# Four down-projection operands made one by one inside the next block, and the second logits product over all 128 rows

## The chip, the core and the metric

The kernel runs on one core of one Trainium2 chip. Its time is the device time of one launch in microseconds (us). The kernel before took 2153.45 us, the median of three runs (2152.48 to 2155.72). The engines are named as in the profile: PE is TensorE (PEld its weight loads), DVE is VectorE, ACT is ScalarE, POOL is GpSimd, and SP is SyncE, which issues the DMAs.

## The reference: one layer of a decoder trunk

The input x is 512 tokens of 2048 float32 values. What is computed, cut to what matters:

```python
h = rmsnorm(x, norm_mix)
proj = h @ w_in                                   # split into the inputs of three head groups
out_a = rmsnorm(swa_sink_attention(aq, ak, av, sinks, rel_bias))   # 12 heads, 4 key/value heads, window 128
out_b = rmsnorm(gla_chunked(bq, bk, bv, log_gate)) * silu(br)      # 4 heads, gated linear attention
out_c = rmsnorm(stick_breaking_attention(cq, ck, cv))              # 8 heads, strictly causal
x = x + concat(out_a, out_b, out_c) @ w_out
h = rmsnorm(x, norm_mlp)
x = x + square(relu(h @ w_mlp_in)) @ w_mlp_out    # 2048 -> 8192 -> 2048
out = rmsnorm(x, norm_final)
```

The heads are 64 wide. The logits of the two softmax-like groups are `q @ k.T` over these 64 values: `z` in the stick-breaking group, `logits` in the window group.

## The kernel before

**Products in parts.** Every float32 operand is split into a high part, rounded to the format that PE multiplies (`whi`, `sh`, `kh`), and a low part, the rest (`wlo`, `sl`, `kl`). ACT makes the high part by a copy, DVE the low part by a subtraction. A product is then three matmuls: high by high, high by low, low by high. The large products (query and key columns of the stick-breaking group, output projection, both MLP projections) go by a Strassen-like scheme with seven products per two-by-two block, named A11, S1, S2, A12, S3, S4 and A22; the sums of blocks that it needs are made by DVE (L174 is the helper `sub`, L171 `add`).

**Logits.** A head's 64 query rows and its 64 key rows are each loaded twice, into the lower and the upper 64 partitions (`twice`, L516). `split_q` (L522) leaves the high part of q in the lower half of `qh` and the low part in the upper half. `split_k` (L530) makes `kh`, the high part of k, on all 128 partitions, and `kl`, the low part, on the lower 64. `qk` (L537) then needs two matmuls: L539 multiplies all 128 rows of `qh` by `kh`, which sums the high and the low part of q against the high part of k; L540 multiplies the lower 64 rows of `qh` by `kl`. It is called once for each stick-breaking head and 128-query block (8 heads, 4 blocks, 256 to 512 key columns), followed there by a bf16 matmul that adds the mask (L564), and once for each window head and block (12 heads, 4 blocks, 256 key columns): 80 calls in all. `split_k` runs 12 times (8 stick-breaking heads and 4 key/value heads).

**Stages.** Input transposes and the first projections come first. The stick-breaking heads run in a software pipeline of six steps per head and block (load, split, logits, weights, transpose, values), beside the matmuls of other projections (L119 to L121); then the gated group; then the window heads in a like pipeline, beside the first output-projection products (L958 to L960). After them come the rest of the output projection, the up-projection (16 blocks `b` of 512 columns, L1261 to L1263) and the down-projection (8 groups `g`, L958 to L960).

**Down-projection operands.** Two up-projection blocks make the operands of one down-projection group. The results of a block are four tiles `a[i, j]` (tile name `av`). `down_half` (L1229) makes seven operands of them: A11 and S3 when the first block is done, A12 in the second block, and, when the second block is done, A22, S1, S2 and S4, one behind the other. `down_split` (L1221) makes one: a copy on ACT (L1224, `dh`), a subtraction on DVE (L1225, `dl`), and two DMAs to HBM (L1226, L1227), from which the down-projection reads them back (L1339). The parts `dh` and `dl` share a ring of two buffers.

**What sets the order.** The kernel is written with a tile framework. Its scheduler takes the instructions in the order of the program text, with their priorities (`tc.high_priority()` moves loads and weight splits ahead), their dependencies and the free buffers of each pool, and lays down one fixed list for each engine. Each engine works its list in order and waits on semaphores; where something stands on an engine is thus decided at build time.

Of the kernel before, what the change touches and what calls it, by code (L numbers as in the profile page):

```python
# [10 lines left out]
F32 = mybir.dt.float32  # L11
F32R = mybir.dt.float32r
# [3 lines left out]
ALU = mybir.AluOpType  # L16
# [7 lines left out]
HD = 64  # L24
# [39 lines left out]
def trunk(ctx, tc, x, norm_mix, w_in, sinks, rel_bias, gate_w, gate_b, gla_norm,  # L64
          swa_norm, sb_norm, w_out, norm_mlp, w1, w2, norm_final, hconst, honehot, out):
    nc = tc.nc
    V, S, G, T = nc.vector, nc.scalar, nc.gpsimd, nc.tensor
# [102 lines left out]
    def add(out_, a, b, eng=G):  # L170
        eng.tensor_tensor(out=out_, in0=a, in1=b, op=ALU.add)  # L171

    def sub(out_, a, b, eng=G):
        eng.tensor_tensor(out=out_, in0=a, in1=b, op=ALU.subtract)  # L174

    ORDER = ("A11", "S1", "S2", "A12", "S3", "S4", "A22")

    ORDER0 = ("A11", "A12", "S1", "S2", "S4", "S3", "A22")
# [91 lines left out]
    def qkh(name, shape=(P, 512), dt=F32):  # L270
        return own("qkh", 6, name, shape, dt)
# [24 lines left out]
    for q in range(4):  # L296
# [7 lines left out]
        for a in range(4):  # L304
# [3 lines left out]
            g = gT[:, 4 * q + a : 4 * q + a + 1]  # L308
# [137 lines left out]
    for g in range(2):  # L446
        sops = hops[g]
# [81 lines left out]

    def split_k(raw):  # L530
        kh = qkh("kh", dt=F32R)
        kl = qkh("kl", (HD, 512), F32R)
        S.activation(kh, raw, AF.Copy)
        V.tensor_tensor(out=kl, in0=raw[:HD], in1=kh[:HD].bitcast(F32), op=ALU.subtract)
        return kh, kl

    def qk(z, qh, qs, k, ks, last=True):  # L537
        kh, kl = k
        T.matmul(z, lhsT=qh[:, qs], rhs=kh[:, ks], start=True, stop=False, skip_group_check=True)  # L539
        T.matmul(z, lhsT=qh[:HD, qs], rhs=kl[:, ks], start=False, stop=last, skip_group_check=True)  # L540


    hd, oC = {}, {}
# [392 lines left out]
    def slot(pool, name, shape, dt=F32):  # L936
        return pool.tile(list(shape), dt, tag="s", name=name)
# [3 lines left out]

    def row_group(acc, sops, wsrc, k1, k2, done=None, order=ORDER, rscale=None, before=None):
        for np_ in range(2):
            raws = raw_tiles([wsrc[k : k + 512, n * 1024 + np_ * 512 : n * 1024 + np_ * 512 + 512]
                              for k in (k1, k2) for n in range(2)], rp)

            def quad(i, j, h):
                return raws[2 * (i - 1) + j - 1][:, 2 * h : 2 * h + 2]  # L950

            def mm(dst, s, wt, h, start, rows):
                (sh, sl, _), (wh, wl) = s, wt
                for u in rows:
                    us = slice(u * P, (u + 1) * P)
                    for k in range(2):
                        kc = 2 * h + k
                        T.matmul(dst[u], lhsT=sh[:, kc, us], rhs=wh[:, k], start=start and k == 0, stop=False, skip_group_check=True)  # L958
                        T.matmul(dst[u], lhsT=sh[:, kc, us], rhs=wl[:, k], start=False, stop=False, skip_group_check=True)  # L959
                        T.matmul(dst[u], lhsT=sl[:, kc, us], rhs=wh[:, k], start=False, stop=h == 1 and k == 1, skip_group_check=True)  # L960

            def after(p, X, Y, Z, rows):
                todo = {"A11": (X, 0, 0), "S1": (Z, 1, 1), "S2": (X, 0, 1), "A12": (Y, 0, 0),
                        "S3": (X, 1, 1), "S4": (Z, 0, 1), "A22": (X, 1, 0)}[p]
                bk, th, nh = todo
                for u in rows:
                    a = acc[2 * th + u][nh][:, np_ * 512 : np_ * 512 + 512]
                    if rscale:
                        V.scalar_tensor_tensor(out=a, in0=bk[u], scalar=rscale[2 * th + u], in1=a, op0=ALU.mult, op1=ALU.add)  # L969
                    else:  # L970
                        V.tensor_tensor(out=a, in0=bk[u], in1=a, op=ALU.add)
                if done:
                    done(p, np_, rows)

            strassen(quad, sops, mm, 2, after, order, None if np_ else before, by_rows=done and np_)


# [82 lines left out]
    with tc.high_priority():  # L1060
        sops, ready = mixed_operands(1536, 1024, lambda n: slot(s3, n, (P, 2, 512)), lambda n: slot(s1, n, (P, 2, 512)))
# [5 lines left out]
    acc = load_acc(lambda t, nh: x[t * P : (t + 1) * P, nh * 1024 : (nh + 1) * 1024])  # L1067
    row_group(acc, sops, w_out, 1536, 1024, before=first_ops)
    sops, ready = mixed_operands(0, 512)
# [135 lines left out]
    NG = DFF // 1024  # L1205
# [15 lines left out]
    def down_split(g, p, t, last=False):  # L1221
        hi = tp4.tile([P, 4, 256], F32R, tag="t1", name="dh", bufs=2)
        lo = t.bitcast(F32R) if last else tp4.tile([P, 4, 256], F32R, tag="t1", name="dl", bufs=2)
        S.activation(hi, t, AF.Copy)  # L1224
        V.tensor_tensor(out=lo, in0=t, in1=hi.bitcast(F32), op=ALU.subtract)  # L1225
        nc.sync.dma_start(dS[g][p][0], hi.bitcast(F32))  # L1226
        nc.sync.dma_start(dS[g][p][1], lo.bitcast(F32))  # L1227

    def down_half(b, th):  # L1229

        g, j = divmod(b, 2)
        a = quads
        if (j, th) == (0, 0):
            down_split(g, "A11", a[1, 1])
        elif (j, th) == (0, 1):
            sub(a[1, 1], a[1, 1], a[2, 1], V)
            down_split(g, "S3", a[1, 1])
        elif (j, th) == (1, 0):
            down_split(g, "A12", a[1, 2])
        else:  # L1240
            down_split(g, "A22", a[2, 2])
            add(a[2, 1], a[2, 1], a[2, 2], V)
            down_split(g, "S1", a[2, 1], True)
            sub(a[1, 1], a[2, 2], a[1, 1], V)
            down_split(g, "S2", a[1, 1])
            sub(a[1, 2], a[1, 2], a[1, 1], V)
            down_split(g, "S4", a[1, 2], True)

    for b in range(DFF // 512):
        raws = raw_tiles([w1[k * 512 : (k + 1) * 512, b * 512 : (b + 1) * 512] for k in range(4)], rp)  # L1250

        def wquad(i, j, h):
            return raws[2 * (i - 1) + h][:, :, (j - 1) * 256 : j * 256]

        def mm(dst, s, wt, h, start, rows):
            (sh, sl, _), (wh, wl) = s[h], wt
            for j in range(2):
                js = slice(j * P, (j + 1) * P)
                o = dst[0][:, j * 256 : (j + 1) * 256]
                for k in range(4):  # L1260
                    T.matmul(o, lhsT=wh[:, k, js], rhs=sh[:, k], start=start and j == 0 and k == 0, stop=False, skip_group_check=True)  # L1261
                    T.matmul(o, lhsT=wh[:, k, js], rhs=sl[:, k], start=False, stop=False, skip_group_check=True)  # L1262
                    T.matmul(o, lhsT=wl[:, k, js], rhs=sh[:, k], start=False, stop=h == 1 and k == 3, skip_group_check=True)  # L1263

        down_quads(b)
        done = []

        def view(th, nh):
            return quads[th + 1, b % 2 + 1][:, 2 * nh : 2 * nh + 2]

        def finish(th, nh):
            v = view(th, nh)
            S.activation(v, v, AF.Square)
            if th in done:
                down_half(b, th)
            done.append(th)

        def after(p, X, Y, Z, rows):
            bk = {"S1": Z, "S4": Z, "A12": Y}.get(p, X)[0].rearrange("p (j q) -> p j q", j=2)
            th, nh, first = {"A11": (0, 0, 1), "S1": (1, 1, 1), "S2": (0, 1, 1), "A12": (0, 0, 0),  # L1280
                             "S3": (1, 1, 0), "S4": (0, 1, 0), "A22": (1, 0, 1)}[p]
            v = view(th, nh)
            if p == "A22":
                S.activation(v, bk, AF.Relu)
            elif first:
                S.copy(v, bk)
            else:
                V.tensor_tensor(out=v, in0=bk, in1=v, op=ALU.add)
                S.activation(v, v, AF.Relu)
            if not first or p == "A22":  # L1290
                finish(th, nh)

        strassen(wquad, up_ops, mm, 1, after, *((ORDER0, up_operand) if b == 0 else ()), ahead=b > 0)
# [38 lines left out]
    r2 = [row_rms2(xsq, t) for t in range(NT)]  # L1332
# [10 lines left out]
    for g in range(NG):  # L1343
        sops = down_operands(g)
        if g == 0:
            acc = load_acc(lambda t, nh: dx2[t][nh])
        if g == NG - 1:
            pool = places.pop(0)
            for nh in range(2):
                gt = slot(pool[nh], "gfin", (P, 1024))  # L1350
                nc.sync.dma_start(gt, bcast(norm_final[nh * 1024 : (nh + 1) * 1024], 1024))
                gfin.append(gt)
        row_group(acc, sops, w2, g * 1024, g * 1024 + 512, *((y_done, ORDER0) if g == NG - 1 else (None, ORDER)), rscale=r2)


# [31 lines left out]
```

## Time and profile before

| | us |
|---|---|
| median of three runs | 2153.45 |
| the profiled execution, whole | 2151.19 |
| its span, first to last instruction | 2149.4 |
| PE busy in the span | 2076.6 (97%) |
| DVE busy | 1664.7 (77%) |
| ACT busy | 1039.8 (48%) |
| POOL busy | 97.7 (5%) |

The profile is of one execution. A matmul's shown end is modelled and the next one may start before it, so the pace of PE is read from one start to the next rather than from durations. "64\*128" in a row is the part of the PE array that an instruction uses, rows by columns. "x2" is two instructions merged into a row. In a list of waits, the engine that stood idle comes first, and what it waited for second. The mean granted clock of PE over the span is 0.988 of full speed.

### The profile page before, as it was taken

To read this page: it belongs to the slowest core of one execution; us is meant where nothing else is said; L and a number is where in the kernel's file an instruction comes from. 1 tells how busy PE (TensorE), PEld (TensorE's weight loads), DVE (VectorE), ACT (ScalarE), POOL (GpSimd) and SP (SyncE) were. 2 spreads that over 40 slices of the span, in tenths; PEclk is the share of its full clock that TensorE was granted. 3 is DMA by queue.
4 is the path that set the end of the run, shared out by engine and by line. 5 is a ranking of instruction groups with operands and counts; after the bars stand their busy time and mean duration, and the time that the engine had idled before them with its cause. 6 is when DMAs were issued, how large, how long until landed. Compare 5 with 4: busy or idle time off the path is not lost. (4 is left out here: it accounts for less than half of the span.)

```text
span 2149.4 us, 30666 instructions
## 1 busy us (share of the span) xinstructions
PE 2076.6 (97%) x12174; PEld 1786.0 (83%) x12174; DVE 1664.7 (77%) x1936; ACT 1039.8 (48%) x1500; POOL 97.7 (5%) x63
## 2 busy tenths in 40 slices
PE   8999999999899997999999999999999999999997
PEld 7997877777677776999999999999788888888876
DVE  7875554435677898788888888887998988988887
ACT  6435644323365465565565565555433333333334
POOL 1110000011200002000000000000000000000012
PEclk9999999999999999999999999999999999999999
DMA  6375333334532442464464554569766366455532
GB/s 227 114 173 147 109 126 106 120 116 146 182 103 82 164 143 83 157 236 177 176 224 179 186 206 181 190 217 374 264 229 241 136 218 234 167 205 216 196 117 79
DMA packets 180906, 373.17 MB, mean 174 GB/s; under 512 B 19800, under 2 KB 44186, under 8 KB 180762
## 3 DMA queue, kind: packets, MB, share of 16 engines
q1 hardware_dynamic: 180762, 371.20, 49.7%
q8 instruction: 96, 1.57, 0.3%
q14 instruction: 48, 0.39, 0.1%
HBM read 287.01 MB, written 84.15 MB: 173 GB/s over the span
## 5 line engine op out<-in xcount | busy, mean ns | idle before, releaser
L200 ACT ACTIVATE whi<-raw 128x1024 fp32r<-128x1024 f32 x532 | 561.7, 1060 | 682.5 <-PE X L960 239.5
L201 DVE TENSOR_TENSOR wlo<-raw,whi 128x1024 fp32r<-128x1024 f32 x532 | 647.2, 1227 | 152.6 <-ACT whi L200 152.0
L174 DVE TENSOR_TENSOR raw<-raw 128x1024 f32<-128x1024 f32 x304 | 369.8, 1230 | 31.0 <-DMA raw<-in_w_mlp_in 25.3
L1263 PE MATMUL X<-sh,wlo 128*128 128x256 f32 x1024 | 290.3, 284 | 10.8 <-DVE wlo L201 10.8
L1261 PE MATMUL X<-sh,whi 128*128 128x256 f32 x1024 | 289.9, 283 | 11.0 <-ACT whi L200 10.0
L1262 PE MATMUL X<-sl,whi 128*128 128x256 f32 x1024 | 288.3, 282 | 0.0
L959 PE MATMUL X<-wlo,sh 128*128 128x512 f32 x640 | 257.1, 402 | 2.8 <-DVE wlo L201 2.7
L960 PE MATMUL X<-whi,sl 128*128 128x512 f32 x640 | 256.1, 400 | 0.0
L958 PE MATMUL X<-whi,sh 128*128 128x512 f32 x640 | 233.8, 402 | 11.5 <-ACT whi L200 4.3
L1263 PEld LDWEIGHTS X<-sh,wlo 128*128 128x128 f32 x1024 | 195.2, 191 | 14.1 <-DVE wlo L201 14.1
L1261 PEld LDWEIGHTS X<-sh,whi 128*128 128x128 f32 x1024 | 195.4, 191 | 13.3 <-ACT whi L200 12.0
L1262 PEld LDWEIGHTS X<-sl,whi 128*128 128x128 f32 x1024 | 195.3, 191 | 0.0
L958 PEld LDWEIGHTS X<-whi,sh 128*128 128x128 f32 x640 | 121.3, 190 | 42.6 <-issue 6.2
L959 PEld LDWEIGHTS X<-wlo,sh 128*128 128x128 f32 x640 | 122.1, 191 | 33.6 <-DVE wlo L201 5.2
L960 PEld LDWEIGHTS X<-whi,sl 128*128 128x128 f32 x640 | 122.0, 191 | 28.8
L1262 PE MATMUL Z<-sl,whi 128*128 128x256 f32 x512 | 143.1, 280 | 2.3 <-DVE sl L1106 2.3
L1261 PE MATMUL Z<-sh,whi 128*128 128x256 f32 x512 | 143.3, 280 | 0.2 <-ACT whi L200 0.2
L1263 PE MATMUL Z<-sh,wlo 128*128 128x256 f32 x512 | 142.8, 279 | 0.0
L959 PE MATMUL Z<-wlo,sh 128*128 128x512 f32 x320 | 127.0, 397 | 0.3 <-DVE wlo L201 0.3
L960 PE MATMUL Z<-whi,sl 128*128 128x512 f32 x320 | 126.6, 396 | 0.0
L958 PE MATMUL Z<-whi,sh 128*128 128x512 f32 x320 | 115.3, 398 | 2.1 <-DVE acc L969 1.1
L113 DVE TENSOR_TENSOR wlo<-raw,whi 128x1024 fp32r<-128x1024 f32 x64 | 80.6, 1261 | 44.0 <-ACT whi L112 42.2
(345 smaller groups left out, 4014.5 us busy)
## 6 DMA issues: line engine op xcount, KB each, us to landing
raw<-in_w_mlp_in SPq DMA_DIRECT2D x64, 1024.0 KB, 6.2
raw<-in_w_mlp_out SPq DMA_DIRECT2D x64, 1024.0 KB, 5.9
raw<-in_w_in SPq DMA_DIRECT2D x28, 1024.0 KB, 5.0
raw<-in_w_out SPq DMA_DIRECT2D x16, 1024.0 KB, 5.0
raw<-in_w_in SPq DMA_DIRECT2D x8, 768.0 KB, 4.8
xt<-in_x SPq DMA_DIRECT2D x16, 256.0 KB, 7.4
raw<-in_w_in SPq DMA_DIRECT2D x8, 512.0 KB, 8.9
raw<-daqk SPq DMA_DIRECT2D x32, 128.0 KB, 2.7
```

What stands on the lines that cost most here:

```text
L113: V.tensor_tensor(out=lo, in0=part, in1=hi.bitcast(F32), op=ALU.subtract)
L174: eng.tensor_tensor(out=out_, in0=a, in1=b, op=ALU.subtract)
L200: S.activation(hi, half, AF.Copy)
L201: V.tensor_tensor(out=lo, in0=half, in1=hi.bitcast(F32), op=ALU.subtract)
L958: T.matmul(dst[u], lhsT=sh[:, kc, us], rhs=wh[:, k], start=start and k == 0, stop=False, skip_group_check=True)
L959: T.matmul(dst[u], lhsT=sh[:, kc, us], rhs=wl[:, k], start=False, stop=False, skip_group_check=True)
L960: T.matmul(dst[u], lhsT=sl[:, kc, us], rhs=wh[:, k], start=False, stop=h == 1 and k == 1, skip_group_check=True)
L1261: T.matmul(o, lhsT=wh[:, k, js], rhs=sh[:, k], start=start and j == 0 and k == 0, stop=False, skip_group_check=True)
L1262: T.matmul(o, lhsT=wh[:, k, js], rhs=sl[:, k], start=False, stop=False, skip_group_check=True)
L1263: T.matmul(o, lhsT=wl[:, k, js], rhs=sh[:, k], start=False, stop=h == 1 and k == 3, skip_group_check=True)
```

## The change

`split_k` makes `kl` on all 128 partitions, and L540 multiplies all 128 rows of `qh` by it, so that the low part of q meets the low part of k as well. The four operands that `down_half` makes at the end of a group's second block become a list of four steps; a step is taken after each product but A11 of the next block (`after`), or, for the last group, after products of the first down-projection group (`row_group`, by the new argument `spare`).

```diff
     def split_k(raw):
         kh = qkh("kh", dt=F32R)
-        kl = qkh("kl", (HD, 512), F32R)
+        kl = qkh("kl", dt=F32R)
         S.activation(kh, raw, AF.Copy)
-        V.tensor_tensor(out=kl, in0=raw[:HD], in1=kh[:HD].bitcast(F32), op=ALU.subtract)
+        V.tensor_tensor(out=kl, in0=raw, in1=kh.bitcast(F32), op=ALU.subtract)
...
-        T.matmul(z, lhsT=qh[:HD, qs], rhs=kl[:, ks], start=False, stop=last, skip_group_check=True)
+        T.matmul(z, lhsT=qh[:, qs], rhs=kl[:, ks], start=False, stop=last, skip_group_check=True)
...
+                if spare:
+                    spare()
                 if done:
                     done(p, np_, rows)
...
-            down_split(g, "A22", a[2, 2])
-            add(a[2, 1], a[2, 1], a[2, 2], V)
-            down_split(g, "S1", a[2, 1], True)
-            sub(a[1, 1], a[2, 2], a[1, 1], V)
-            down_split(g, "S2", a[1, 1])
-            sub(a[1, 2], a[1, 2], a[1, 1], V)
-            down_split(g, "S4", a[1, 2], True)
+            q = dict(a)
+
+            def s1_step():
+                add(q[2, 1], q[2, 1], q[2, 2], V)
+                down_split(g, "S1", q[2, 1], True)
...
+            later_steps.extend([lambda: down_split(g, "A22", q[2, 2]), s1_step, s2_step, s4_step])
...
+    def next_step():
+        if later_steps:
+            later_steps.pop(0)()
...
         def after(p, X, Y, Z, rows):
+            if p != "A11":
+                next_step()
...
-        row_group(acc, sops, w2, g * 1024, g * 1024 + 512, *((y_done, ORDER0) if g == NG - 1 else (None, ORDER)), rscale=r2)
+        row_group(acc, sops, w2, g * 1024, g * 1024 + 512,
+                  *((y_done, ORDER0) if g == NG - 1 else (None, ORDER)), rscale=r2, spare=next_step)
```

On DVE, in the stick-breaking stage, the low parts of two heads' keys stand like this, before (-) and with the change (+); `raw` is the loaded key, `qh` the split query, `e` belongs to the weights of a head:

```order
 L526 SCALAR_TENSOR_TENSOR qh<-raw_1541,qh 64x512
 L113 TENSOR_TENSOR wlo<-raw,whi 128x1024
-L534 TENSOR_TENSOR kl<-raw_1544,kh 64x512
+L534 TENSOR_TENSOR kl<-raw_1544,kh 128x512
 L526 SCALAR_TENSOR_TENSOR qh<-raw_1594,qh 64x512
-L534 TENSOR_TENSOR kl<-raw_1597,kh 64x512
+L534 TENSOR_TENSOR kl<-raw_1597,kh 128x512
 L573 SCALAR_TENSOR_TENSOR e<-z,e 128x128
```

The subtraction is made at the same place on twice the partitions; this holds for all 12.

On ACT, at the end of the first group, these are the copies of the four operands (`dh`) in the kernel before. Of the `av` tiles, 7678 is A22, 7187 becomes S1, 7186 becomes S2 and 7677 becomes S4; `av_8135` and `av_8136` are the results of the next block, whose weights are the `raw` tiles 8127 to 8133:

```order
L1224 ACTIVATE dh_8102<-av_7678 128x1024
L200 ACTIVATE whi_8201<-raw_8129 128x1024
L1286 COPY av_8135<-X_8147 128x512
L200 ACTIVATE whi_8257<-raw_8127 128x1024
L1224 ACTIVATE dh_8109<-av_7187 128x1024
L1224 ACTIVATE dh_8115<-av_7186 128x1024
L1286 COPY av_8136<-Z_8207 128x512
L200 ACTIVATE whi_8261<-raw_8129 128x1024
L200 ACTIVATE whi_8316<-raw_8131 128x1024
L200 ACTIVATE whi_8320<-raw_8133 128x1024
L1224 ACTIVATE dh_8122<-av_7677 128x1024
```

With the change the same stretch of ACT's list reads (buffer and line numbers differ, since tiles are numbered in the order of the text; the next block's tiles are now 8110 and 8111, its weights 8102 to 8108):

```order
L1226 ACTIVATE dh_8231<-av_7678 128x1024
L200 ACTIVATE whi_8176<-raw_8104 128x1024
L1305 COPY av_8110<-X_8122 128x512
L200 ACTIVATE whi_8238<-raw_8102 128x1024
L1226 ACTIVATE dh_8297<-av_7187 128x1024
L1226 ACTIVATE dh_8363<-av_7186 128x1024
L1305 COPY av_8111<-Z_8182 128x512
L200 ACTIVATE whi_8242<-raw_8104 128x1024
L200 ACTIVATE whi_8303<-raw_8106 128x1024
L200 ACTIVATE whi_8307<-raw_8108 128x1024
L1226 ACTIVATE dh_8429<-av_7677 128x1024
```

Nothing has moved there. Line and buffer numbers apart, the lists of all five engines, 1354 rows on ACT and 670 on SP among them, are the same before and with the change, but for the 12 subtractions above, the waits of DVE that go with their upper halves, and the rows of the array that L540 uses.

## Rows read from the trace of the kernel before

**Rows 1.** The page: span, and busy time of the engines.
```profile
span 2149.4 us, 30666 instructions
...
PE 2076.6 (97%) x12174; PEld 1786.0 (83%) x12174; DVE 1664.7 (77%) x1936; ACT 1039.8 (48%) x1500; POOL 97.7 (5%) x63
```

**Rows 2.** Busy time by stretch: us, each engine's busy us (instructions), PEclk, DMA share, GB/s.
```profile
163.00:390.00 227.00, 227.00 (x1089) 180.27 (x1088) 121.93 (x197) 118.14 (x246) 0.00 (x0) 1.00 0.38 118
540.00:666.00 126.00, 117.24 (x604) 89.74 (x603) 88.79 (x222) 64.04 (x179) 15.07 (x7) 0.96 0.41 134
900.00:1200.00 300.00, 292.68 (x2463) 289.60 (x2462) 248.58 (x224) 177.26 (x209) 0.00 (x0) 0.99 0.54 197
1200.00:1500.00 300.00, 294.55 (x2450) 291.24 (x2449) 246.12 (x223) 178.30 (x210) 0.00 (x0) 0.99 0.61 224
```

**Rows 3.** Line 540: ns minimum/median/maximum, first and last start, forms.
```profile
L540 PEld LDWEIGHTS z<-kl,qh x80: 182/183/285, 164.9 to 665.1; 64*128 64x128 f32 x80
L540 PE MATMUL z<-kl,qh x80: 379/382/579, 164.9 to 665.1; 64*128 64x256 f32 x64, 64*128 64x384 f32 x8, 64*128 64x512 f32 x8
```

**Rows 4.** Timeline of PE, stick-breaking stage: start us, us, engine, line, operation, tiles.
```profile
164.09 0.40 PE L539 MATMUL z<-kh,qh 128*128 128x256 f32 x2
164.32 0.40 PE L121 MATMUL acc<-whi,hT1l 128*128 128x512 f32 x1
164.56 0.40 PE L119 MATMUL acc<-whi,hT1h 128*128 128x512 f32 x1
164.88 0.38 PE L540 MATMUL z<-kl,qh 64*128 64x256 f32 x1
165.20 0.23 PE L564 MATMUL z<-negb,identb 128*128 128x128 bf16 x1
165.36 0.38 PE L540 MATMUL z<-kl,qh 64*128 64x256 f32 x1
165.67 0.23 PE L564 MATMUL z<-negb,identb 128*128 128x128 bf16 x1
165.71 0.48 PE L120 MATMUL acc<-wlo,hT1h 128*128 128x512 f32 x1
```

**Rows 5.** Timeline of the weight loads in the same stretch.
```profile
163.86 0.42 PEld L539 LDWEIGHTS z<-kh,qh 128*128 128x128 f32 x2
...
164.88 0.18 PEld L540 LDWEIGHTS z<-kl,qh 64*128 64x128 f32 x1 [0.37 <-issue]
```

**Rows 6.** Timeline of PE, window stage.
```profile
635.03 0.36 PE L539 MATMUL z<-kh,qh 128*128 128x256 f32 x1
635.33 0.38 PE L540 MATMUL z<-kl,qh 64*128 64x256 f32 x1
635.64 0.39 PE L539 MATMUL z<-kh,qh 128*128 128x256 f32 x1
635.95 0.38 PE L540 MATMUL z<-kl,qh 64*128 64x256 f32 x1
636.26 0.66 PE L872 MATMUL ptp<-ident,L 128*128 128x128 f32 x4
```

**Rows 7.** Waits, 163 to 390 us: who waited for whom, us, times, longest.
```profile
ACT e L566 <- PE z L564: 54.0, 16, 5.3
```

**Rows 8.** Waits, 540 to 666 us.
```profile
ACT L L864 <- DVE nm L856: 17.6, 8, 7.9
...
PE z L539 <- DVE oa L904: 5.5, 1, 5.5
```

**Rows 9.** Line 534.
```profile
L534 DVE TENSOR_TENSOR kl<-raw,kh x12: 676/684/686, 160.1 to 619.9; 64x512 fp32r<-64x512 f32 x12
```

**Rows 10.** Groups of DVE, 100 to 800 us: count, busy us, mean ns, idle before.
```profile
L989 DVE TENSOR_TENSOR sl<-tp,sh 128x512 fp32r<-128x512 f32 x28 | 18.3, 682 | 1.9 <-ACT sh L988 1.8
```

**Rows 11.** Timeline of PE after a stall, window stage.
```profile
590.95 0.63 PE L959 MATMUL X<-wlo,sh 128*128 128x512 f32 x1
591.37 0.63 PE L960 MATMUL X<-whi,sl 128*128 128x512 f32 x1
```

More of the change, by code (lines that the diff above doesn't have):

```diff
@@ L940, in trunk, with row_group @@
     nbank[0] = -1
-    def row_group(acc, sops, wsrc, k1, k2, done=None, order=ORDER, rscale=None, before=None):
+    def row_group(acc, sops, wsrc, k1, k2, done=None, order=ORDER, rscale=None, before=None, spare=None):
         for np_ in range(2):
@@ L1240, in down_half, with s2_step, s4_step @@
         else:
-            down_split(g, "A22", a[2, 2])
-            add(a[2, 1], a[2, 1], a[2, 2], V)
-            down_split(g, "S1", a[2, 1], True)
-            sub(a[1, 1], a[2, 2], a[1, 1], V)
-            down_split(g, "S2", a[1, 1])
-            sub(a[1, 2], a[1, 2], a[1, 1], V)
-            down_split(g, "S4", a[1, 2], True)
+            q = dict(a)
+            def s1_step():
+                add(q[2, 1], q[2, 1], q[2, 2], V)
+                down_split(g, "S1", q[2, 1], True)
+            def s2_step():
+                sub(q[1, 1], q[2, 2], q[1, 1], V)
+                down_split(g, "S2", q[1, 1])
+            def s4_step():
+                sub(q[1, 2], q[1, 2], q[1, 1], V)
+                down_split(g, "S4", q[1, 2], True)
+            later_steps.extend([lambda: down_split(g, "A22", q[2, 2]), s1_step, s2_step, s4_step])
+    later_steps = []
+    def next_step():
+        if later_steps:
+            later_steps.pop(0)()
     for b in range(DFF // 512):
```

## The prediction

> **What bounds the kernel now.** I read the page first [rows 1]: PE is busy for 97% of the span, DVE for 77%, so what is not on PE's own path can hardly move the end. Then the busy time by stretch, at the three places that the change touches [rows 2]. In the stick-breaking stage (163 to 390 us) PE has no idle time at full clock, DVE and ACT are about half busy, and in the list of waits it is ACT that waits for the logits, 54.0 us in 16 waits [rows 7]; PE's list alone sets the pace there. In the window stage (540 to 666 us) PE is busy for 117.2 of 126 us and DVE for 88.8; a stall of 5.5 us on DVE is seen, and ACT waits 17.6 us for DVE [rows 2, 8]: here two engines share the bound. In the middle of the up-projection (900 to 1500 us) PE is idle for 600 − 292.68 − 294.55 = 12.8 us [rows 2].
>
> Last I read PE's timeline instruction by instruction around the line that changes. "Busy" hides what is to be seen there: full-array products follow each other smoothly, and every step into and out of a 64-row product is long.
>
> **The change part by part.**
>
> *The four operands made one by one: 0 us.* The text moves them; the built program doesn't. In ACT's list the copies of A22, S1, S2 and S4 stood among the next block's weight splits before, and stand at the same places now (the two lists in the section on the change); PE, POOL and SP read the same throughout, so the eight DMAs of the four operands are issued from the same places and pass nothing on SP's queue, and no wait is added. The scheduler had already spread them, since the text gives only a priority and the ring of two `dh`/`dl` buffers forces a step-by-step pace in either version. If this reading were wrong, the most that could be had is the whole idle time of PE in the middle of the up-projection, 12.8 us [rows 2].
>
> *The subtraction on all 128 partitions: 0 us.* Twelve subtractions of 64x512 take 684 ns each [rows 9]; one of 128x512 of the same kind, though from PSUM, takes 682 ns [rows 10]. Bounds: −0.1 and, if it took as long as twice the rows, +0.68 us each, 8.2 us in all on an engine that is half idle in the first of the two stages. I take 0, from the nearest row. The subtraction now reads the upper half of the loaded key and so depends on that DMA too. Behind it in DVE's list stand the next query's low part, a weight split and the weights of a head, and PE would wait for all of these; but it already waits for `kh`, which ACT makes from the same 128 rows, so the upper half has landed by then. The buffer for `kl` comes from the ring in which `kh` and `qh` take 128 partitions anyway.
>
> *The second logits product on 128 rows: the whole effect.* There are 80 of them, 64 with 256 columns, 8 with 384 and 8 with 512 [rows 3]. The pace of full-array products: two L539 of 256 columns stand in 164.32 − 164.09 = 0.23 us, so 0.115 us each, and one of 512 columns takes 164.56 − 164.32 = 0.24 [rows 4]. Now the 64-row ones. In the window stage four products of 256 columns, L539, L540, L539, L540, take 636.26 − 635.03 = 1.23 us [rows 6]; at 0.115 they would take 0.46. So two L540 cost 0.77 us extra, 0.385 each: about half on the way in (635.33 − 635.03 = 0.30 instead of 0.115), half on the way out (0.31 instead of 0.115). In the stick-breaking stage, two L540 with their mask products: in 0.32 instead of 0.24, out 0.32 instead of 0.115, in 0.16 instead of 0.04 (a mask product followed by a full-array one: 165.71 − 165.67), out 0.31 instead of 0.115, together 0.60 extra, 0.30 each [rows 4]. There the weight load shows why: L540's load begins at 164.88, with the product itself, and PEld stood idle for 0.37 us before it, while the load of the two L539 began at 163.86, 0.23 us ahead of the first product [rows 4, 5]. A product over a different number of rows waits until the array has emptied, and its weights aren't loaded ahead.
>
> With 128 rows both steps fall away. Bounds per product: 0.30 and 0.385 us. Wider ones (384, 512 columns) pay the same on each side, as they take longer for other reasons.
>
> Stick-breaking stage, 32 products: 9.6 to 12.3 us. PE sets the pace alone there, and ACT's 54.0 us of waits are for these very products, so all of it is on the path. Most of the products stand right behind their L539, as in rows 6 and not as in rows 4; I take 0.36, 11.5 us.
>
> Window stage, 48 products, all of the kind in rows 6: 48 × 0.385 = 18.5 us on PE. How much reaches the end lies between 0 (the waits for DVE grow by as much) and 18.5. PE is busy for 93% of the stretch, which alone would leave 17.2; but short waits hide under the modelled ends of matmuls, and the chain from logits over DVE's maximum, ACT's exponential, PE's transpose and ACT's copy back to PE passes two other engines. I take two thirds, 12.3 us. What is late next there is DVE: 88.8 of 126 us become 88.8 of 114.
>
> Sum: −11.5 − 12.3 = −23.8 us. Behind these stages the program is the same and starts that much earlier. The profiled execution took 2151.19 us, 1.8 more than its span and 2.3 less than the median; by its own account the new time is 2127.4, and against the median 2153.45 − 23.8 = **2129.7 us**.
>
> **The rivals.**
>
> *All of it reaches the end.* 80 × 0.385 = 30.8: 2122.6 us. For it: PE is nearly always busy in both stages. Against it: the 5.5 us stall of PE for DVE, and ACT's 17.6 us for DVE [rows 8].
>
> *The window stage gives nothing back.* DVE, and ACT behind it, would set the pace there: 2153.45 − 11.5 = 2141.9 us. For it: the same waits. Against it: DVE is busy for 70% of the stretch, so PE's list must hold it up somewhere.
>
> *The steps don't fall away, because a full-array weight load can't run under a full-array product.* Each product next to L540 would then wait for its load: 0.2 us of load [rows 5] and 0.115 of product make 0.315, against 0.30 and 0.31 now, so nothing would be won: 2153.5, within 0.2%. Against it: the two L539, each with a load of about 0.2 us, stand 0.115 us apart, both on the full array [rows 4, 5]; loads do run under products there. The Trainium skill, "TensorE: Matmul & The Clock Gate", section "The mechanism" (under "What overlaps and what doesn't"), says that a weight load overlaps products in flight only when it goes to other rows of the array. By that rule this rival would win; the trace disagrees, with 0.115 us from start to start.
>
> *Slower: PE runs ahead of its inputs and its clock falls.* After the stall in the window stage, products of 512 columns start 591.37 − 590.95 = 0.42 us apart instead of 0.24 [rows 11]: half the clock, 1.2 instead of 2.4 GHz. The same in the stick-breaking stage, if a faster PE came to wait for DVE and ACT between heads: every us of products done at half clock costs one more. Its 227 us are now at clock 1.00 [rows 2]; a quarter of them at half clock, some 55 us, would cost 55 − 23.8 = 31 net: 2185 us. It decides from 24 us of such products on. Against it: in that stage PE is waited for and waits for nobody.
>
> *The operands do move.* Up to 12.8 us more: 2117. The lists speak against it.
>
> **How the numbers follow.** The forecast has 0.64, all of it at the end 0.17, nothing from the window stage 0.11, no effect of the rows 0.04, slower 0.02, and moved operands 0.02. What a measurement of this kernel can tell from no change is about 0.2%, 4.3 us. Only the case without effect lies within that, so same has 0.04, slower 0.02 and faster 0.94. The forecast's own spread (a half to five sixths of the window stage) is 2126 to 2133; the range reaches to the full gain on one side and almost to the bare stick-breaking gain on the other: 2122 to 2140.
>
> **What would show it.** L540 in the form 128\*128, with a weight load that begins ahead of its product; four products of the kind in rows 6 in about 0.5 us instead of 1.23; the up-projection's first instruction some 24 us earlier, of which about 11 are already there at the end of the stick-breaking stage; `kl` still at about 0.68 us; the same idle time of PE, about 6 us in 300, in the middle of the up-projection. The prediction is wrong if L540 still starts 0.30 us after L539, if the window stage ends no earlier than the stick-breaking stage's gain explains, or if PE's clock drops between 163 and 390 us.

## The result, and the profile after

| | before | after |
|---|---|---|
| median, us | 2153.8 (2152.48 to 2155.72, 4 runs) | 2132.28 (2129.26 to 2134.56, 4 runs) |
| the profiled execution, us | 2151.19 | 2129.26 |
| its span, us | 2149.4 | 2127.5 |

A fourth run of the kernel before came with the result, so its median is 2153.8 here. The changed kernel is faster: ratio 0.9899, 95% interval 0.9881 to 0.9916, or −21.5 us by the medians. 2129.7 was predicted, within 2122 to 2140. The two profiled spans differ by 21.9 us, and everything below is a search for these.

The page of the changed kernel, against [rows 1]:

```profile
span 2127.5 us, 30668 instructions
...
PE 2050.9 (96%) x12174; PEld 1778.3 (84%) x12174; DVE 1665.9 (78%) x1936; ACT 1038.6 (49%) x1500; POOL 97.8 (5%) x63
```

PE runs as many products as before in 25.7 us less of busy time; the other engines do what they did. Line 540 of the changed kernel, against [rows 3]:

```profile
L540 PEld LDWEIGHTS z<-kl,qh x80: 187/192/333, 165.6 to 643.2; 128*128 128x128 f32 x80
L540 PE MATMUL z<-kl,qh x80: 277/282/415, 165.9 to 643.4; 128*128 128x256 f32 x64, 128*128 128x384 f32 x8, 128*128 128x512 f32 x8
```

The form is now 128\*128. From the first product of the line to the last it was 665.1 − 164.9 = 500.2 us, and is 643.4 − 165.9 = 477.5: 22.7 less. Behind the last it was 2149.4 − 665.1 = 1484.3 us to the end, and is 2127.5 − 643.4 = 1484.1. So the whole gain was made between the first and the last product of this line.

How, PE's timeline of the changed kernel shows at the place of [rows 4]:

```profile
165.17 0.40 PE L539 MATMUL z<-kh,qh 128*128 128x256 f32 x2
165.41 0.40 PE L121 MATMUL acc<-whi,hT1l 128*128 128x512 f32 x1
165.64 0.40 PE L119 MATMUL acc<-whi,hT1h 128*128 128x512 f32 x1
165.88 0.28 PE L540 MATMUL z<-kl,qh 128*128 128x256 f32 x1
166.00 0.23 PE L564 MATMUL z<-negb,identb 128*128 128x128 bf16 x1
166.04 0.36 PE L540 MATMUL z<-kl,qh 128*128 128x256 f32 x1
166.24 0.23 PE L564 MATMUL z<-negb,identb 128*128 128x128 bf16 x1
166.28 0.48 PE L120 MATMUL acc<-wlo,hT1h 128*128 128x512 f32 x1
...
616.12 1.00 PE L890 MATMUL oA<-av,pT 128*128 128x64 f32 x8
616.93 0.36 PE L539 MATMUL z<-kh,qh 128*128 128x256 f32 x1
617.13 0.28 PE L540 MATMUL z<-kl,qh 128*128 128x256 f32 x1
617.25 0.28 PE L539 MATMUL z<-kh,qh 128*128 128x256 f32 x1
617.37 0.28 PE L540 MATMUL z<-kl,qh 128*128 128x256 f32 x1
617.49 0.60 PE L872 MATMUL ptp<-ident,L 128*128 128x128 f32 x4
617.93 0.33 PE L890 MATMUL oA<-av,pT 128*128 128x64 f32 x2
```

Read the starts. In the upper piece a mask product now follows its L540 after 166.00 − 165.88 = 0.12 us, where it took 0.32; from the first L121 to L120 it is 0.87 us instead of 1.39. In the lower piece, the window stage, the four products take 617.49 − 616.93 = 0.56 us instead of 1.23 [rows 6], and the steps of 0.30 to 0.31 have become 0.20, 0.12, 0.12 and 0.12. The weight loads of the changed kernel, against [rows 5]:

```profile
165.41 0.19 PEld L119 LDWEIGHTS acc<-whi,hT1h 128*128 128x128 f32 x1
165.65 0.19 PEld L540 LDWEIGHTS z<-kl,qh 128*128 128x128 f32 x1
...
616.90 0.19 PEld L539 LDWEIGHTS z<-kh,qh 128*128 128x128 f32 x1
617.01 0.19 PEld L540 LDWEIGHTS z<-kl,qh 128*128 128x128 f32 x1
```

L540's load begins 0.23 us ahead of its product, under L119's; before, it began with the product itself.

By stretch, against [rows 2]:

```profile
163.00:390.00 227.00, 227.00 (x1132) 185.35 (x1131) 126.89 (x203) 120.04 (x249) 0.53 (x1) 1.00 0.39 123
...
900.00:1200.00 300.00, 292.72 (x2462) 289.62 (x2462) 252.28 (x226) 179.06 (x211) 0.00 (x0) 0.99 0.54 200
1200.00:1500.00 300.00, 290.00 (x2344) 283.22 (x2343) 246.25 (x224) 170.84 (x201) 0.00 (x0) 0.98 0.62 230
```

In the stick-breaking stage PE still has no idle time and the clock is still 1.00: the same stretch holds 43 more of PE's products. The window stage is cut by its own bounds, from its first L539 to its last, since it ends 22 us earlier; first before, then after:

```profile
545.50:664.70 119.20, 110.44 (x567) 85.61 (x565) 86.93 (x220) 63.05 (x175) 15.07 (x7) 0.96 0.38 124
537.70:643.20 105.50, 93.24 (x567) 79.11 (x566) 87.79 (x219) 62.61 (x175) 15.14 (x7) 0.97 0.42 139
```

DVE is busy there for 87.8 of 105.5 us, 83% instead of 73%, and PE's idle time has grown from 119.20 − 110.44 = 8.8 to 105.50 − 93.24 = 12.3 us.

The stages themselves, from the first L539 to the last L564 or L539 of each in the two timelines: stick-breaking 220.15 us before, 211.28 after, −8.9; between the two 161.3 in both, of which the gated stage, from its first L691 on, takes 127.1; the window stage 119.2 before, 105.5 after, −13.7. Together −22.6.

The waits of the changed kernel between 163 and 390 us, against [rows 7]:

```profile
ACT e L566 <- PE z L564: 46.5, 14, 4.8
```

ACT waits 7.5 us less for the logits. The same view between 540 and 645 us, against [rows 8]:

```profile
ACT L L864 <- DVE nm L856: 19.8, 11, 7.9
...
PE z L539 <- DVE oa L904: 5.5, 1, 5.5
```

PE's own stall for DVE in the window stage is what it was, and ACT waits 2.2 us more for DVE.

### The profile page after: what moved, and what is told of

It is laid out like the page before. It is cut to its first block, busy times and chain, and to the rows that moved or that the text cites. A ratio compares the mean times of both kernels' runs of the same rounds, so it can differ in the third digit from the quotient of the medians.

```text
span 2127.5 us, 30668 instructions
## 1 busy us (share of the span) xinstructions
PE 2050.9 (96%) x12174; PEld 1778.3 (84%) x12174; DVE 1665.9 (78%) x1936; ACT 1038.6 (49%) x1500; POOL 97.8 (5%) x63
## 5 line engine op out<-in xcount | busy, mean ns | idle before, releaser
L1278 PEld LDWEIGHTS X<-sh,whi 128*128 128x128 f32 x1024 | 196.5, 192 | 13.3 <-ACT whi L200 12.1
```

## The experiments

**The rows alone.** The kernel before, with `kl` and L540 on 128 rows and nothing else of the change.

```diff
-        kl = qkh("kl", (HD, 512), F32R)
+        kl = qkh("kl", dt=F32R)
-        V.tensor_tensor(out=kl, in0=raw[:HD], in1=kh[:HD].bitcast(F32), op=ALU.subtract)
+        V.tensor_tensor(out=kl, in0=raw, in1=kh.bitcast(F32), op=ALU.subtract)
-        T.matmul(z, lhsT=qh[:HD, qs], rhs=kl[:, ks], start=False, stop=last, skip_group_check=True)
+        T.matmul(z, lhsT=qh[:, qs], rhs=kl[:, ks], start=False, stop=last, skip_group_check=True)
```

> The kernel before with the second logits product on 128 rows, and the four operands made as before. Theory (all of the gain is the rows of this product): as fast as the changed kernel, 0.990 of before, 2129 to 2135 us. Rival (the four operands gave part of it): slower than the changed kernel by that part, up to 0.996 of before if they gave 12.8 us.

2134.12 us against 2156.26 of before, measured beside it, ratio 0.9898 (0.9886 to 0.9910): the whole gain.

**The steps alone.** The changed kernel with these three lines put back.

> The changed kernel with the second logits product back on 64 rows, and the four operands as steps in the next block. Theory: its lists are those of before in every row, so no change, 0.998 to 1.002 of before. Rival (the steps save waits in the up-projection): up to 12.8 us less, 0.994 of before, and less than 6 us of idle PE in 300 in the middle of the up-projection.

2158.01 us, ratio 1.0002 (0.9994 to 1.0011): nothing. Its up-projection by stretch, beside 292.68 and 294.55 us of PE in [rows 2]:

```profile
900.00:1200.00 300.00, 292.70 (x2464) 289.83 (x2464) 249.95 (x225) 177.41 (x210) 0.00 (x0) 1.00 0.52 193
1200.00:1500.00 300.00, 294.02 (x2465) 291.42 (x2464) 243.24 (x220) 176.52 (x208) 0.00 (x0) 0.99 0.60 220
```

**The steps really moved.** In the changed kernel the steps are taken later, so that the built lists do change, and S4's copy lands in the block after the next.

```diff
-            if p != "A11":
+            if p not in ("A11", "S1", "S2"):
                 next_step()
```

> The changed kernel with the four steps taken after A12, S3, S4 and A22 of the next block instead of S1, S2, A12 and S3; here the lists do move: the copy of S4 leaves its place among the weight splits and stands a block later. Theory (what is moved costs DVE and ACT the same, and waits of 1.8 us for each group stay): the time of the changed kernel within 0.2%, 0.988 to 0.992 of before. Rival (the four operands crowd out weight splits): up to 6 us less, 0.987. Rival (later writes hold the ring of two buffers longer): 2 to 6 us more, 0.992 to 0.993.

2158.04 us (2144.53 to 2163.07), ratio to before 1.0010 (0.9996 to 1.0025): the gain is gone, some 24 us against the changed kernel. ACT's timeline of this kernel in the up-projection shows the place (in square brackets the idle time ahead and what ended it):

```profile
949.32 1.06 ACT L1226 ACTIVATE dh<-av 128x1024 fp32r<-128x1024 f32 x1 [3.86 <-DMA dS1A<-dh]
...
954.37 0.59 ACT L1305 COPY av<-X 128x512 f32<-128x512 f32 x1 [0.50 <-DMA dS0S<-av]
```

PE's timeline of the same stretch:

```profile
952.34 0.28 PE L1279 MATMUL Z<-sl,whi 128*128 128x256 f32 x1
955.01 0.45 PE L1278 MATMUL X<-sh,whi 128*128 128x256 f32 x1 [2.39 <-ACT av L1305]
955.26 0.42 PE L1279 MATMUL X<-sl,whi 128*128 128x256 f32 x1
955.47 0.42 PE L1280 MATMUL Z<-sh,wlo 128*128 128x256 f32 x1
```

And the waits of this kernel between 860 and 1560 us:

```profile
PE X L1278 <- ACT av L1305: 10.2, 6, 2.4
```

The chain has two links. First S4's copy (949.32) waits 3.86 us for a buffer of the ring, which an operand of the next group (`dS1A`) still holds. Then S4's low part, written over its own tile, leaves by DMA from there; the next group's result, which ACT copies out of PE's bank at L1305, needs that tile's buffer and waits 0.50 us for the DMA. PE waits for the bank, and afterwards its products start 0.22 us apart instead of 0.12: the granted clock was 0.53 from 955.0 to 958.4. In ACT's list a wait for the ring, of 1.05 to 4.18 us, stands ahead of all six of PE's waits, a wait of L1305 for the DMA ahead of five. The changed kernel's trace has no such wait for L1305. The whole up-projection, from the start of its first product to that of its last, in the kernel before, in the changed kernel and in this one:

```profile
821.70:1494.70 673.00, 644.99 (x5384) 637.35 (x5383) 554.85 (x506) 395.27 (x468) 15.79 (x4) 0.99 0.53 195
799.80:1475.50 675.70, 647.35 (x5385) 639.70 (x5384) 555.61 (x507) 395.33 (x469) 15.80 (x4) 0.98 0.53 194
799.20:1502.50 703.30, 661.07 (x5385) 650.72 (x5384) 553.61 (x506) 393.19 (x470) 15.76 (x4) 0.97 0.51 185
```

It takes 27.6 us more than in the changed kernel; PE is idle for 703.30 − 661.07 = 42.2 us in it, against 28.3, and the clock is lower. The theory on record falls; its rival, by which the ring is held longer, had the direction and the first link, but a price several times too small. So the steps cost nothing in the change because the built lists stay as they were, and not because their place doesn't matter.

**The subtraction alone.** `kl` on 128 partitions, L540 on the lower half of it.

```diff
-        T.matmul(z, lhsT=qh[:HD, qs], rhs=kl[:, ks], start=False, stop=last, skip_group_check=True)
+        T.matmul(z, lhsT=qh[:HD, qs], rhs=kl[:HD, ks], start=False, stop=last, skip_group_check=True)
```

> The kernel before with the low part of the key made on all 128 partitions, and the product still on 64 rows of it. Theory: the subtraction costs the same, 0.68 us, and hides, so no change, 0.998 to 1.002 of before. Rival (the wider subtraction, or its wait for the upper half, costs): 12 times up to 0.68 us, 8 us more, 1.004 of before, or a longer wait of DVE ahead of it.

2156.13 us, ratio 0.9993 (0.9983 to 1.0002). Its line 534, against [rows 9]:

```profile
L534 DVE TENSOR_TENSOR kl<-raw,kh x12: 682/693/693, 160.1 to 619.1; 128x512 fp32r<-128x512 f32 x12
```

9 ns more each, twelve times.

**One stage at a time.** L540 on 128 rows in the stick-breaking stage only, then in the window stage only (`last` is false in the first; the window run has `P if last else HD`).

```diff
+        r = slice(0, P if not last else HD)
-        T.matmul(z, lhsT=qh[:HD, qs], rhs=kl[:, ks], start=False, stop=last, skip_group_check=True)
+        T.matmul(z, lhsT=qh[r, qs], rhs=kl[r, ks], start=False, stop=last, skip_group_check=True)
```

> 128 rows in the stick-breaking stage alone (32 products), 64 in the window stage. Theory from the traces of before and after (0.092 us on the way in, 0.191 on the way out, all on PE's path): 8.9 us less than before, 0.9959 of it. Rival (0.36 each, as predicted): 11.5 us, 0.9947. Rival (the stage gives back what it gains): no change.

> 128 rows in the window stage alone (48 products), 64 in the stick-breaking stage. Theory from the traces of before and after (16.4 us on PE, 2.2 of them given back as waits): 14.2 us less than before, 0.9934 of it. Rival (two thirds of 18.5, as predicted): 12.3 us, 0.9943; the two are too close to be told apart by the time, so the trace decides. Rival (the window stage gains only when the stage before it has moved): under 5 us.

Stick-breaking only: 2146.45 us, ratio 0.9956 (0.9942 to 0.9970). Window only: 2142.26 us, 0.9937 (0.9924 to 0.9950). 0.44% and 0.63% make 1.07%, the whole gain within the intervals. Over the stage as measured above, each profiled kernel that has 128 rows there (or 96, below) shortens it by 8.8 to 9.8 us, and each that has not takes 220.15. The window stage varies more: 103.7 to 108.8 us in nine profiles with 128 or 96 rows there (mean 106.52), 118.3 to 119.6 in four with 64 rows, each behind its L539 (mean 118.86), 12.3 less. Its length goes with the clock: among the nine, the granted clock over the stage was 0.97 in the five that took 103.7 to 105.8 us and 0.94 in the four that took 107.7 to 108.8.

**The 64 rows kept, the steps halved.** In the window stage both L539 first, then both 64-row products. The second L539 opens the shared bank before the first half is closed, so the sums of the first half come out changed; instructions and shapes are the same.

```diff
-            qk(z[:, u * 256 : (u + 1) * 256], qh, slice(i * P, (i + 1) * P), kv[h // 3][0], slice(k0, k0 + 256))
+            T.matmul(z[:, u * 256 : (u + 1) * 256], lhsT=qh[:, i * P : (i + 1) * P], rhs=kv[h // 3][0][0][:, k0 : k0 + 256],
+                     start=True, stop=False, skip_group_check=True)
+        for u in range(2):
...
+            T.matmul(z[:, u * 256 : (u + 1) * 256], lhsT=qh[:HD, i * P : (i + 1) * P], rhs=kv[h // 3][0][1][:, k0 : k0 + 256],
+                     start=False, stop=True, skip_group_check=True)
```

> The kernel before, 64-row products as they were, but in the window stage the two L539 of a step stand side by side, and the two 64-row products behind them, so that 48 of 160 steps between the forms fall away and no product changes. Theory (a step between forms costs, not the product): in the window stage 24 times 0.28 to 0.37 us less, 6.7 to 8.9 us, 2145 to 2147 us; two 64-row products in a row start 0.12 to 0.2 us apart. Rival (each 64-row product is slow by itself, its load cannot be ahead): 0.30 us from one 64-row product to the next, and no gain, 2152 to 2155 us.

2147.25 us, ratio 0.9954 (0.9942 to 0.9966). PE's timeline of this kernel, window stage:

```profile
630.20 0.48 PE L847 MATMUL z<-kh,qh 128*128 128x256 f32 x2
630.62 0.50 PE L852 MATMUL z<-kl,qh 64*128 64x256 f32 x2
631.04 0.66 PE L878 MATMUL ptp<-ident,L 128*128 128x128 f32 x4
```

The four products take 631.04 − 630.20 = 0.84 us, between 1.23 and 0.56, with two switches of form instead of four. The second 64-row product starts at 630.84, 0.22 us behind the first: a little more than the 0.12 to 0.2 expected, and less than the 0.30 of the rival. The price belongs to the switch, not to the 64-row product. The Trainium skill, "TensorEngine Tiling (Array Packing)", section "Key Properties", says that a change of the tiling mode drains TensorE, without a figure; this trace agrees.

**Products of 96 rows.** The changed kernel, with

```diff
-        T.matmul(z, lhsT=qh[:, qs], rhs=kl[:, ks], start=False, stop=last, skip_group_check=True)
+        T.matmul(z, lhsT=qh[:96, qs], rhs=kl[:96, ks], start=False, stop=last, skip_group_check=True)
```

> The second logits product over 96 of the 128 rows (the low part of q then meets the low part of k for half of the 64 values), four operands as before. Theory (what costs is the change between array forms of 64 and 128 rows, and 96 rows run in the form of 128, as the 96-row products of the gated stage do, 0.232 us behind a 512-column product): as fast as on 128 rows, 0.988 to 0.992 of before, and 0.12 us from it to the next product. Rival (any product on other rows than its neighbour makes the array empty first): 0.30 us on both sides, and the time of before.

2132.23 us against 2152.17 of before, ratio 0.9907 (0.9890 to 0.9923), and PE's timeline of it has the pace of 128 rows:

```profile
165.12 0.28 PE L540 MATMUL z<-kl,qh 96*128 96x256 f32 x1
165.24 0.23 PE L564 MATMUL z<-negb,identb 128*128 128x128 bf16 x1
```

**Low part first.** In the changed kernel L539 takes `kl` and L540 takes `kh`, to see whether the 0.20 us that is left between the first L539 and L540 belongs to the low part or to the place.

```diff
-        T.matmul(z, lhsT=qh[:, qs], rhs=kh[:, ks], start=True, stop=False, skip_group_check=True)
-        T.matmul(z, lhsT=qh[:, qs], rhs=kl[:, ks], start=False, stop=last, skip_group_check=True)
+        T.matmul(z, lhsT=qh[:, qs], rhs=kl[:, ks], start=True, stop=False, skip_group_check=True)
+        T.matmul(z, lhsT=qh[:, qs], rhs=kh[:, ks], start=False, stop=last, skip_group_check=True)
```

> 128 rows everywhere, four operands as before, but the product with the low part of the key stands first and the one with the high part second. Theory (behind a transpose or a values product the first of the two has its start noted some 0.08 us early, whichever it is): 0.20 us from the first to the second, 0.12 behind the second, as in the changed kernel with the roles exchanged, and its time, 2129 to 2139 us. Rival (the product with the low part has a wait of its own): 0.12 from the first to the second, or a longer step ahead of the first.

One run, 2134.56 us. PE's timeline, window stage:

```profile
619.08 0.37 PE L539 MATMUL z<-kl,qh 128*128 128x256 f32 x1
619.28 0.28 PE L540 MATMUL z<-kh,qh 128*128 128x256 f32 x1
619.40 0.28 PE L539 MATMUL z<-kl,qh 128*128 128x256 f32 x1
```

The 0.20 stays with the first place, behind the short products.

**The same remedy elsewhere.** In the gated stage the state products (L751) also use half the array. First with both chunks' rows in each product, so that the chunks aren't separated:

```diff
-  T.matmul(dsp[:DK, us], lhsT=ke[cs, h * DK : (h + 1) * DK], rhs=vt[cs, us], start=True, stop=True)
+  T.matmul(dsp[:DK, us], lhsT=ke[:, h * DK : (h + 1) * DK], rhs=vt[:, us], start=True, stop=True)
```

> The changed kernel with the gated group's state products (line 751, 56 instructions of 64 rows by 96 columns) over all 128 rows; this sums both chunks of a block and so leaves their separation out. Theory (the same two steps, 0.09 us in and 0.09 out, at some 10 places in the trace after the change): 1.2 to 1.9 us less between 430 and 540 us of the span, and 0.16 from such a product to the next of another form instead of 0.25. Rival (the steps cost for the logits alone, for example because their two products share a bank and an operand): no change in that stage.

One run, 2129.42 us; the gated stage shrinks from 127.07 to 123.62 us, 3.45 less, where 1.2 to 1.9 was expected. PE's timeline of the changed kernel at that place:

```profile
444.50 0.89 PE L751 MATMUL dsp<-bva,ke 64*96 64x192 f32 x4
...
445.97 0.50 PE L120 MATMUL acc<-hT1l,whi 128*128 128x512 f32 x1
```

And of this one:

```profile
444.68 0.87 PE L751 MATMUL dsp<-bva,ke 128*96 128x192 f32 x4
...
445.91 0.53 PE L120 MATMUL acc<-hT1l,whi 128*128 128x512 f32 x1
```

The 56 products stand in ten groups of four or eight, so a visit to the other form is paid ten times: 3.45 / 10 = 0.345 us each, where 0.09 in and 0.09 out were expected. Eight stand together at the place shown, and from the first of them to L120 it is 1.47 us against 1.23. PE has no idle time in this stage and its clock is 1.00, in both. Then with the separation kept, by masked copies of `ke` that DVE makes in place of a product on POOL:

```diff
-  G.tensor_tensor(out=ke, in0=st["bk"], in1=ke, op=ALU.mult)
+  V.scalar_tensor_tensor(out=ke1, in0=ke, scalar=ind[:, 1:2], in1=st["bk"], op0=ALU.mult, op1=ALU.mult)
+  V.scalar_tensor_tensor(out=ke, in0=ke, scalar=ind[:, 0:1], in1=st["bk"], op0=ALU.mult, op1=ALU.mult)
...
+  T.matmul(dsp[:DK, us], lhsT=ke[c][:, h * DK : (h + 1) * DK], rhs=vt[:, us], start=True, stop=True)
```

> The changed kernel, and the state products over 128 rows with the right result: the key operand is made twice by DVE, each with the rows of the other chunk set to zero (8 instructions of 128x384 more on DVE, 4 fewer on POOL). Theory (the steps between array forms are worth 3.4 us in the gated stage, as the run that left the chunks unseparated showed, and DVE, about half busy there, hides the 8 instructions): 2 to 3.5 us less than the changed kernel, 0.988 to 0.9885 of before. Rival (DVE's chain to the state becomes late, PE waits for it): no gain or up to 4 us more than the changed kernel.

> The changed kernel once more on the same chip as the run before it, for the comparison of the two: 0.9899 of before, between 0.988 and 0.9916.

2129.06 us with the masks, the changed kernel again, beside it, 2133.32, before 2158.91: ratios 0.9867 (0.9845 to 0.9889) and 0.9883 (0.9863 to 0.9903). The gated stage takes 123.43 us, 3.6 less. The medians say that this version beats the changed kernel by 4.3 us, and the stage agrees; the intervals overlap, so the ratio alone doesn't show it.

## Why the prediction was right, step by step

*The four operands, 0 us:* right; the steps alone give 1.0002. The expected idle time of PE in the middle of the up-projection, 12.8 us in the two stretches, came out as 600 − 292.72 − 290.00 = 17.3. With the same steps and 64 rows it is 13.3, so the steps don't make it. The two stretches now hold a part of the program that stood 22 us later. Over the whole up-projection, in the rows shown with the moved steps, PE is idle for 673.00 − 644.99 = 28.0 us before and 675.70 − 647.35 = 28.3 after, so nothing was added to speak of. Why the scheduler makes one list out of both texts is also open: a longer ring of `dh`/`dl` was not tried.

*The subtraction, 0 us:* right, 692 ns against 684, and 0.9993 alone.

*The product on 128 rows, the whole effect:* right; the rows alone give the whole ratio, and both switches shrink. One sentence of it is too wide: that a product over a different number of rows waits until the array has emptied. Products of 64 rows do; those of 96 rows don't, and the next one starts 0.12 us behind them. The rival by which a full-array load can't run under a product is out: the load begins 0.23 us ahead.

*The stick-breaking term, −11.5 us:* the step that was mis-sized. It gave −8.9, 0.277 us per product and not 0.36, below even the lower bound of 0.30. I took the price from [rows 6] because most L540 stand right behind their L539. But in [rows 6] the first step, 0.30 us, was compared with a pace of 0.115; the changed kernel and the swapped one both keep 0.20 there with no switch at all. A product behind short ones (L890, a transpose, or the mask product) has its start noted some 0.08 us early, and the next step looks longer by that. The loads agree: in the changed kernel the load of the L539 behind L890 begins at 616.90, 0.03 us ahead of its product's noted start, and that of the next L540 at 617.01, 0.12 ahead. So a switch into 64 rows shows as 0.30 − 0.20 = 0.10 there, and as 0.31 − 0.12 = 0.19 only where the L539 ahead follows another L540; the way out shows as 0.31 − 0.12 = 0.19, or 0.31 − 0.20 = 0.11 for the L540 behind a mask product in [rows 4]. Summed over all starts of the two traces, the stick-breaking stage wins 3.0 us on the way in and 6.1 on the way out, (3.0 + 6.1) / 32 = 0.28. The nearer rows were [rows 4], from the stage itself: their two products together save 1.39 − 0.87 = 0.52, 0.26 each.

*The window term, −12.3 us:* right, and the share in part by luck. On PE the steps in and out shrink by 7.0 and 9.4 us. The step behind the way out shrinks too, which it doesn't in the stick-breaking stage (from a mask product to the next 0.04 us in both). In the kernel before, behind [rows 6], stand these, the first of PE and the second of its loads:

```profile
636.76 0.78 PE L890 MATMUL oA<-av,pT 128*128 128x64 f32 x6
636.26 0.43 PEld L872 LDWEIGHTS ptp<-ident,L 128*128 128x128 f32 x4
```

From the first L872 to L890 it is 636.76 − 636.26 = 0.50 us, and 617.93 − 617.49 = 0.44 in the changed kernel; the load of that L872 begins with its noted start, so this start is early as well. At 21 of the 24 places where a run of these products ends, this step is 0.05 to 0.11 us shorter after the change; over all of them but one, where the clock of the kernel before had fallen, it is 1.8 us. So the rows were worth 7.0 + 9.4 + 1.8 = 18.2 us on PE, and the 18.5 on record was about right: in [rows 6] the early start of the first product and that of the last nearly cancel. Of the 18.2, 13.7 reached the end in the two profiles and 12.3 in the mean over all, 75 and 68%. The two thirds had been chosen between bounds and not worked out. New idle time of PE, 12.3 − 8.8 = 3.5 us, is most of what was given back. DVE was not yet the bound at 83% busy, and PE's stall for it stayed at 5.5 us.

*The sum, −23.8 us:* −22.7 between the first and last product of the line, −21.9 over the span, −21.5 by the medians. In the profiles, the stick-breaking term was 2.6 us too large and the window term 1.4 too small, and the changed kernel's first product of the line stood 1.0 us later (165.9 against 164.9), which comes from the start of that execution, ahead of anything that the change touches. *Slower by the clock:* no; it stays at 1.00 in the stick-breaking stage, and PE is still the engine waited for.

## What to carry to other kernels

A product over half the rows amid full ones costs no less PE time than a full one and pays two switches of form, here 0.28 us a visit in the stick-breaking stage, 0.345 in the gated one and 18.2 / 48 = 0.38 in the window stage: widen it (96 rows served as well as 128), or put several of the same form together. Price a switch from starts over a run of instructions that reaches to where the steps are alike again, and only against the same place in a program without the switch, since the start behind short products or behind a switch is noted early. Before pricing a step that the text moves, look whether the built lists move; where they do, follow each buffer that the step holds to whoever needs it next.

## What the runs showed of the hardware beyond that

A product of 96 rows is followed after 0.12 us, as one of 128 rows is, and one of 64 after 0.32. How the price of a visit divides between its two switches isn't shown: by the noted starts it is 0.10 to 0.19 us on the way in, 0.19 on the way out and up to 0.11 in the step behind that, but starts there are noted early, as said above. And one wait for a buffer of 2.4 us costs more than itself: behind it products of 256 columns started 0.22 us apart instead of 0.12. The clock fell to half behind three of the six such waits (10.2 us in all); the six went with an up-projection of 703.3 us where the other kernels' take 673 to 679. Of the 27.6 us against the changed kernel, 13.9 are idle time of PE, and how the rest divides no run separates.
